# A gated short-convolution layer on one core: sums of a product with 128 equal columns, an eviction moved ahead of a cast, and the gate's loads moved behind the first stage

## The chip, the core and the metric

The kernel runs on one core of one Trainium2 chip. Five engines matter: TensorE (PE in the profile; PEld is its weight load), VectorE (DVE), ScalarE (ACT), GpSimd (POOL) and SyncE (SP), whose queue issues nearly all DMAs. Each engine works through its own instructions in order and waits for the others at semaphores. The metric is the device time of one execution in microseconds (us); less is better.

## What is computed

One layer on a sequence of 256 rows with 2048 features; everything is float32.

```python
def short_conv_mixer(h, w_in, conv_w, w_out):
    proj = jnp.einsum('bsd,de->bse', h, w_in)            # 2048 -> 4 x 4096
    b_gate, c_gate, v, g = jnp.split(proj, 4, axis=-1)
    u = causal_depthwise_conv(c_gate * v, conv_w)        # width 3
    y = b_gate * u * jax.nn.silu(g)
    return jnp.einsum('bse,ed->bsd', y, w_out)           # 4096 -> 2048

mod = jnp.einsum('bd,df->bf', jax.nn.silu(c), ada_w) + ada_b   # 2048 -> 3 x 2048
shift, scale, gate = jnp.split(mod, 3, axis=-1)
h = rmsnorm(x, norm_g) * (1.0 + scale) + shift
out = rmsnorm(x + gate * short_conv_mixer(h, ...), final_g)
```

Weights are read once: 128 MB of `w_in`, 32 MB of `w_out` and 48 MB of `ada_w`.

## The kernel before, in words

**Precision.** A float32 weight tile of 128 x 2048 (1 MB) is split in two: ScalarE casts it to a rounded part `hi`, VectorE subtracts to get the rest `lo`. The features are split in the same way into `hT` (high and low half). Each product of the layer is three matmuls: hi with high, hi with low, lo with high.

**Preamble (the first 26 us).** x is loaded and transposed on TensorE while `ada_w`'s columns for the first two feature tiles (k = 0 and 1) are loaded in 18 pieces. Their sums over 2048 rows, weighted with silu(c), make shift and scale of these two tiles. VectorE makes 13 of the 16 weighted additions (L391, into `gv0`); TensorE makes the other three (`ON_PE = (7, 11, 13)`, `sum0`, L377) as matmuls whose moving operand is one column, and at last adds `gv0` over the partitions with a column of ones. The results land in `sum0`, VectorE adds the bias (L424, `sh_sc`), ScalarE and VectorE make the features (`features`, L356 to L358), and the first product can start. Between these pieces stand matmuls that compute nothing (`idle`, L280, as many as the table `IDLE` says at eight places); they keep TensorE occupied. Three small loads on POOL's queue bring `norm_g`, all 48 rows of `ada_b` and 96 rows of `conv_w`; two transposes (`tp_v`, L266) turn them, one of them for `cw`, the convolution's taps.

**First stage (26 to 388 us).** It makes half of the projection, while shift and scale of the other 14 feature tiles are still being summed: `ada_w` comes in pieces `at` (512 KB each in two DMAs), VectorE adds them into `gv` (L475), TensorE turns a finished pair of tiles (`tp_g`, L482), ScalarE totals it (L489), VectorE makes scale and shift, and two more features appear in `hT`. The work is cut into 65 blocks (numbered 0 to 64): one weight tile `raw_s`, 48 matmuls (24 in blocks 0 and 1). Most blocks have two halves of 24 matmuls, each into its own PSUM tile (`mm_s`, called a bank in the code), and a pass of one to four blocks fills the same two. Three PSUM buffers rotate: a pass's half can start only when an earlier tile in its buffer has been evicted. Evictions are copies on ScalarE (L529, `acc<-mm_s`) or additions on VectorE (L531); a later pass of the same outputs may start from the evicted sums, which ScalarE copies back (L665, `mm_s<-acc`).

The order of the first stage is written out by the loop over `flat` (L715), with a small clock model that counts each engine's time. In the iteration of block b the loop emits, in this order: the cast `hi` of block b + 2 (L587, through `high`), the eviction of the second half of the pass that ended one block ago (`close_bank(ended_pass, ...)`, L529), some sums, `lo` of block b + 2 (L594), and then block b's matmuls; the first half's eviction is emitted between the two halves. Casts use three `hi` buffers and three `raw` buffers, so a cast waits for its load and for TensorE to leave a buffer. When all features are there, the pinned order ends and the scheduler orders what follows by itself.

**Second stage (388 to 737 us).** The other half of the projection, in 64 tiles of 1 MB with 48 matmuls each (`mm_b`). At every second tile the code issues one of 32 pieces of the gate's part of `ada_w` (`gate_piece`: load `at_g`, 512 KB, L792, and two additions into `gacc`, L799 and L801; after eight pieces TensorE adds over the partitions, `ps_gate`, L808). A lowered priority (`GIVE = 300`) lets the scheduler move them. Nothing they read ties them to the second stage, so it has placed all of them in the first stage's second half.

**Output stage (737 to 918 us).** y times `w_out` in four column groups, with gate, residual and final norm.

Of the kernel before, what the change touches and what calls it, by code (L numbers as in the profile page):

```python
# [49 lines left out]

RAW0 = 23.9
FIRST = 25.2
ISSUE_US = 2.0
TURN_US = 1.0
LOAD_US = 2.65
PIECE_US = 1.47
# [95 lines left out]
def short_conv_layer(ctx: ExitStack, tc: tile.TileContext, x, c, norm_g, ada_w, ada_b, w_in, conv_w, w_out, final_g, out):  # L152
    nc = tc.nc
# [69 lines left out]
    GIVE = 300  # L223
    IDLE = (2, 1, 3, 2, 2, 3, 7, 2)
    xt = [[slot([P, HX], f"x{t}{dh}") for dh in range(2)] for t in range(TT)]
# [8 lines left out]
    NK0 = ADA[0]  # L234
    first_ada = []
# [15 lines left out]
    nc.gpsimd.dma_start(rows1[0:16, :], norm_g.rearrange("o (k p) -> (o k) p", p=P))  # L251
    nc.gpsimd.dma_start(rows1[16:64, :], ada_b.rearrange("o (k p) -> (o k) p", p=P))
    nc.gpsimd.dma_start(rows2[:, :], conv_w.rearrange("w (k p) -> (w k) p", p=P))
    ones_e = const.tile([P, P], F32R, tag="ones", name="ones")
# [4 lines left out]

    vec = const.tile([P, 64], F32, tag="vec", name="vec")  # L260
    cw = const.tile([P, 96], F32, tag="cw", name="cw")
    silu_c = const.tile([P, KT], F32, tag="silu", name="silu_c")

    def turn(rows, lo, n, dst):
        tp = psum.tile([P, 512], F32, tag="sm", name="tp_v", bufs=2)[:, : n - lo]
        nc.tensor.transpose(tp, rows[lo:n, :], ident[lo:n, lo:n])  # L266
        if dst is not None:
            nc.vector.tensor_copy(dst, tp)
        return tp
# [16 lines left out]
    idle(0, turned[2])  # L286
    tp_v = turn(rows1, 0, 64, None)
    gT = vec[:, 0:16]
# [4 lines left out]
    idle(1, turned[2])  # L293
    tp_c = turn(rows2, 0, 96, None)
    idle(2, turned[2])
# [15 lines left out]
    nc.scalar.copy(vec, tp_v)  # L311
    nc.scalar.copy(cw, tp_c)
    nc.vector.tensor_tensor(out=rstd, in0=ssq[:, 0, :], in1=ssq[:, 1, :], op=ALU.add)
# [54 lines left out]

    ON_PE = (7, 11, 13)
    sums0 = [psum.tile([P, 512], F32, tag="sm", name="sum0", bufs=2) for _ in range(NK0)]  # L370
    gv0 = adap.tile([P, 2, 2 * P], F32, tag="gv", name="gv0")[:, :, 0 : NK0 * P]

    def sum0(k, rows, col):

        for f in range(NK0):
            for s in range(2):
                nc.tensor.matmul(  # L377
                    sums0[f][:, s : s + 1], rows[:, s, f * P : (f + 1) * P], col,
                    start=k == ON_PE[0] and s == 0, stop=k is None, skip_group_check=True,
                )  # L380

    def sum0_of(n):
        k = ON_PE[n]
        sum0(k, first_ada[k], silu_c[:, k : k + 1])

# [30 lines left out]
    idle(6, tp_idle)  # L416
    sum0(None, gv0, ones[:, 0:1])
    idle(7, tp_idle)
# [4 lines left out]
    for k in range(NK0):  # L423
        nc.vector.tensor_tensor(out=sh_sc[:, k], in0=sums0[k][:, 0:2], in1=b_both[:, :, k], op=ALU.add)  # L424
    for k in range(NK0):
# [124 lines left out]
    def spend(engine, us, since=0.0):  # L550

        clock[engine] = max(clock[engine], since) + us
        return clock[engine]

    def issue():

        while todo:
            free = [i for i, (kind, item) in enumerate(todo) if not held(kind, item)]
            if not free or free[0] and todo[free[0]][0] == "a":
                return  # L560
            kind, item = todo.pop(free[0])
            if kind == "w":
                _, chs, q, _, _, _, w, s0, sk, _ = flat[item]
                n = sk * w
                col = q * E + chs[0] * CT * P
                raws[item] = raw_tile("raw_s")
                nc.sync.dma_start(
                    raws[item][:, :n].rearrange("p (k f) -> p k f", k=sk),
                    w_in[0, s0 * P : (s0 + sk) * P, col : col + w].rearrange("(k p) f -> p k f", p=P),
                )  # L570
# [9 lines left out]
    def high(b):  # L580

        _, _, _, _, _, _, w, _, sk, _ = flat[b]
        n = sk * w
        while b not in raws:
            sum_one()
        hi = wpool.tile([P, SLOT], F32R, tag="hi", name="hi", bufs=3)
        nc.scalar.copy(hi[:, :n], raws[b][:, :n])  # L587
        spend("act", HI_US * n / SLOT, raws.pop((b, "at")))
        return hi, n, clock["act"]
# [125 lines left out]
    for b, (n, chs, q, k0, k1, seeds, w, s0, sk, _) in enumerate(flat):  # L715
# [257 lines left out]
```

## Time and profile before

| what | value |
|---|---|
| median of three runs | 920.33 us (917.95 to 921.09) |
| the profiled execution's own time | 920.34 us |
| its span on the core | 918.6 us |
| TensorE busy | 900.2 us (98 %) |
| VectorE busy | 632.3 us (69 %) |
| ScalarE busy | 454.1 us (49 %) |
| DMA, mean over the span | 248 GB/s |

In a row of the timeline the columns are start and duration in us, engine, line and operation, the tiles written and read, partitions x elements, the count of instructions merged, and in brackets how long the engine had been idle and what ended the wait. TensorE is busy nearly all the time, so what counts is the few places where it is not, and the 26 us before its first product of the layer.

### The profile page before, as it was taken

To read this page: it belongs to the slowest core of one execution; us is meant where nothing else is said; L and a number is where in the kernel's file an instruction comes from. 1 tells how busy PE (TensorE), PEld (TensorE's weight loads), DVE (VectorE), ACT (ScalarE), POOL (GpSimd) and SP (SyncE) were. 2 spreads that over 40 slices of the span, in tenths; PEclk is the share of its full clock that TensorE was granted. 3 is DMA by queue.
4 is the path that set the end of the run, shared out by engine and by line. 5 is a ranking of instruction groups with operands and counts; after the bars stand their busy time and mean duration, and the time that the engine had idled before them with its cause. 6 is when DMAs were issued, how large, how long until landed. Compare 5 with 4: busy or idle time off the path is not lost.

```text
span 918.6 us, 16218 instructions
## 1 busy us (share of the span) xinstructions
PE 900.2 (98%) x7043; PEld 861.0 (94%) x7043; DVE 632.3 (69%) x603; ACT 454.1 (49%) x431; POOL 2.3 (0%) x9
## 2 busy tenths in 40 slices
PE   7999999999999999999999999999999999999996
PEld 4899999999999999999999999999999988888885
DVE  5888899999988999985545554555454544545882
ACT  6677776545544766543444334433344333443333
POOL 1000000000000000000000000000000000000000
PEclk9999999999999999999999999999999999999999
DMA  9999899999998669876666656665666496555542
GB/s 304 372 382 351 295 355 354 317 351 325 349 337 313 210 216 359 250 247 187 188 197 201 195 183 194 198 204 186 186 192 198 143 343 222 191 203 202 183 138 91
DMA packets 146775, 227.64 MB, mean 248 GB/s; under 512 B 5456, under 2 KB 103808, under 8 KB 146320
## 3 DMA queue, kind: packets, MB, share of 16 engines
q1 hardware_dynamic: 146576, 226.51, 73.1%
q8 instruction: 55, 0.90, 0.4%
q14 instruction: 16, 0.13, 0.0%
q0 software_dynamic: 96, 0.08, 0.0%
q10 hardware_dynamic: 32, 0.01, 0.0%
HBM read 224.49 MB, written 2.10 MB: 247 GB/s over the span
## 4 chain that ended last, share of the span: by engine, by line
PE 92%; DMA 5%; ACT 1%; DVE 1%; issue 0%; ACTq 0%; SPq 0%; DVEq 0%
PE mm_b L497 38%; PE mm_s L497 35%; PE mm_o L869 6%; PE mm_o L871 6%; PE mm_o L870 6%; DMA at<-in_ada_w_dram 2%; DMA raw_s<-in_sc_w_in_dram 2%; DMA at_g<-in_ada_w_dram 1%; ACT hi L587 1%; DMA x<-in_x_dram 1%; DVE lo L594 0%; PE tp_g L482 0%; ACT acc L529 0%; DVE acc L434 0%; DVE gv L475 0%
## 5 line engine op out<-in xcount | busy, mean ns | idle before, releaser
L497 PE MATMUL mm_b<-hT,hi 128*128 128x256 f32 x2048 | 348.4, 276 | 0.0
L497 PE MATMUL mm_s<-hT,hi 128*128 128x256 f32 x2048 | 338.0, 277 | 3.8 <-ACT acc L529 3.8
L497 PEld LDWEIGHTS mm_b<-hT,hi 128*128 128x128 f32 x2048 | 308.2, 188 | 0.0
L497 PEld LDWEIGHTS mm_s<-hT,hi 128*128 128x128 f32 x2048 | 299.9, 188 | 5.0 <-ACT acc L529 4.3
L497 PE MATMUL mm_b<-hT,lo 128*128 128x256 f32 x1024 | 282.6, 276 | 0.0
L497 PE MATMUL mm_s<-hT,lo 128*128 128x256 f32 x1024 | 262.7, 277 | 1.3 <-DVE lo L594 1.3
L365 DVE TENSOR_TENSOR lo<-raw,hi 128x2048 fp32r<-128x2048 f32 x64 | 146.7, 2293 | 133.0 <-ACT hi L364 133.0
L364 ACT CAST hi<-raw 128x2048 fp32r<-128x2048 f32 x64 | 122.5, 1913 | 196.2 <-PE mm_b L497 149.9
L497 PEld LDWEIGHTS mm_b<-hT,lo 128*128 128x128 f32 x1024 | 192.2, 188 | 0.1
L497 PEld LDWEIGHTS mm_s<-hT,lo 128*128 128x128 f32 x1024 | 183.1, 188 | 1.8 <-DVE lo L594 1.7
L587 ACT CAST hi<-raw_s 128x2048 fp32r<-128x2048 f32 (+1 forms) x64 | 121.5, 1900 | 111.5 <-PE mm_s L497 90.7
L594 DVE TENSOR_TENSOR lo<-raw_s,hi 128x2048 fp32r<-128x2048 f32 (+1 forms) x64 | 145.4, 2272 | 19.1 <-ACT hi L587 18.5
L365 DVE TENSOR_TENSOR lo<-raw_o,hi 128x2048 fp32r<-128x2048 f32 x32 | 73.3, 2291 | 64.6 <-ACT hi L364 64.6
L364 ACT CAST hi<-raw_o 128x2048 fp32r<-128x2048 f32 x32 | 61.0, 1907 | 106.8 <-PE mm_o L871 84.8
L870 PE MATMUL mm_o<-lo,y 128*128 128x512 f32 x256 | 99.3, 389 | 0.0
L871 PE MATMUL mm_o<-hi,y 128*128 128x512 f32 x256 | 99.3, 389 | 0.0
L869 PE MATMUL mm_o<-hi,y 128*128 128x512 f32 x256 | 99.3, 389 | 0.0
L475 DVE SCALAR_TENSOR_TENSOR gv<-at,silu_c,gv 128x512 f32<-128x512 f32 x105 | 78.7, 750 | 2.5
L871 PEld LDWEIGHTS mm_o<-hi,y 128*128 128x128 f32 x256 | 48.0, 188 | 10.1
L870 PEld LDWEIGHTS mm_o<-lo,y 128*128 128x128 f32 x256 | 48.0, 188 | 10.0
L869 PEld LDWEIGHTS mm_o<-hi,y 128*128 128x128 f32 x256 | 48.1, 188 | 9.8
L801 DVE SCALAR_TENSOR_TENSOR gacc<-at_g,silu_c,gacc 128x512 f32<-128x512 f32 x60 | 44.9, 748 | 8.7 <-DMA at_g<-in_ada_w_dram 7.9
(107 smaller groups left out, 378.6 us busy)
## 6 DMA issues: line engine op xcount, KB each, us to landing
raw<-in_sc_w_in_dram SPq DMA_DIRECT2D x64, 1024.0 KB, 5.6
raw_s<-in_sc_w_in_dram SPq DMA_DIRECT2D x63, 1024.0 KB, 7.3
raw_o<-in_sc_w_out_dram SPq DMA_DIRECT2D x32, 1024.0 KB, 5.2
at<-in_ada_w_dram SPq DMA_DIRECT2D x126, 256.0 KB, 7.1
at_g<-in_ada_w_dram SPq DMA_DIRECT2D x32, 512.0 KB, 6.3
x<-in_x_dram SPq DMA_DIRECT2D x4, 512.0 KB, 6.5
big<-in_x_dram SPq DMA_DIRECT2D x2, 1024.0 KB, 7.8
out_dram<-big SPq DMA_DIRECT2D x4, 512.0 KB, 2.9
```

The lines of the kernel that those rows point to most:

```text
L364: nc.scalar.copy(hi[:, :n], raw[:, :n])
L365: nc.vector.tensor_tensor(out=lo[:, :n], in0=raw[:, :n], in1=hi[:, :n].bitcast(F32), op=ALU.subtract)
L475: nc.vector.scalar_tensor_tensor(out=gv, in0=at4[:, i], scalar=c_k, in1=gv, op0=ALU.mult, op1=ALU.add)
L497: mm = last_mm[0] = nc.tensor.matmul(dst, w, h[:, k], start=begins and left, stop=ends, skip_group_check=True)
L587: nc.scalar.copy(hi[:, :n], raws[b][:, :n])
L594: nc.vector.tensor_tensor(out=lo[:, :n], in0=raws.pop(b)[:, :n], in1=hi[:, :n].bitcast(F32), op=ALU.subtract)
L801: nc.vector.scalar_tensor_tensor(out=ga, in0=at3[:, i, :], scalar=s, in1=ga, op0=ALU.mult, op1=ALU.add)
L869: nc.tensor.matmul(po, yh, hi[:, o], start=opens, stop=False, skip_group_check=True)
L870: nc.tensor.matmul(po, yh, lo[:, o], start=False, stop=False, skip_group_check=True)
L871: nc.tensor.matmul(po, yl, hi[:, o], start=False, stop=ct == NCT - 1, skip_group_check=True)
```

## The change

Five edits:

1. The first sums on TensorE take 128 equal columns (silu(c)'s column broadcast, or `ones`) as moving operand instead of one; a fourth row tile (k = 15) is summed on TensorE, so VectorE makes 12 additions instead of 13. The two feature tiles' sums are ordered one after the other. The `IDLE` table changes from 22 to 15 matmuls in all.
2. `conv_w`'s rows are loaded and turned after block 44 (`CONV_AT`), on SP's queue; of `ada_b` 32 rows are loaded early instead of 48.
3. The second half's eviction of an ended pass is emitted before the cast of block b + 2 when the model expects that block's load late (`early`).
4. The gate's loads get an ordering dependency on the last `raw_s` load of the first stage.
5. The model's two start times `RAW0` and `FIRST` are 1.0 and 1.2 us less, which moves four of the seven `tp_g` by one block.

```diff
-RAW0 = 23.9
-FIRST = 25.2
+RAW0 = 22.9
+FIRST = 24.0
+EARLY_US = 2.0
+CONV_AT = 44
...
-    IDLE = (2, 1, 3, 2, 2, 3, 7, 2)
+    IDLE = (2, 2, 3, 2, 2, 2, 1, 1)
...
-    nc.gpsimd.dma_start(rows1[16:64, :], ada_b.rearrange("o (k p) -> (o k) p", p=P))
-    nc.gpsimd.dma_start(rows2[:, :], conv_w.rearrange("w (k p) -> (w k) p", p=P))
+    nc.gpsimd.dma_start(rows1[16:48, :], ada_b[0:1, 0 : 2 * D].rearrange("o (k p) -> (o k) p", p=P))
...
-    tp_c = turn(rows2, 0, 96, None)
...
-    nc.scalar.copy(cw, tp_c)
...
-    ON_PE = (7, 11, 13)
-    sums0 = [psum.tile([P, 512], F32, tag="sm", name="sum0", bufs=2) for _ in range(NK0)]
+    ON_PE = (7, 11, 13, 15)
+    sums0 = [psum.tile([P, 2, 2 * P], F32, tag="sm", name="sum0", bufs=2)[:, :, 0:P] for _ in range(NK0)]
...
+        for s in range(2):
+            nc.tensor.matmul(
+                sums0[f][:, s, :], rows[:, s, f * P : (f + 1) * P], cols,
+                start=k == ON_PE[0] and s == 0, stop=k is None, skip_group_check=True,
+            )
+
+    def sum_of(n, f):
+        k = ON_PE[n]
+        sum0(k, f, first_ada[k], silu_c[:, k : k + 1].to_broadcast([P, P]))
...
-    sum0(None, gv0, ones[:, 0:1])
+    for f in range(NK0):
+        sum_of(3, f)
+        sum0(None, f, gv0, ones)
...
-        nxt = b + 2 < N and high(b + 2)
-        if ended_pass is not None:
-            close_bank(ended_pass, len(passes[ended_pass][1]) - 1)
-            ended_pass = None
+        early = b + 2 < N and raws.get((b + 2, "at"), begin) > begin - EARLY_US
+        for closing in (early, not early):
+            if closing:
+                if ended_pass is not None:
+                    close_bank(ended_pass, len(passes[ended_pass][1]) - 1)
+                    ended_pass = None
+            else:
+                nxt = b + 2 < N and high(b + 2)
...
+        if b == CONV_AT:
+            nc.sync.dma_start(rows2[:, :], conv_w.rearrange("w (k p) -> (w k) p", p=P))
+            turn(rows2, 0, 96, cw)
...
-        nc.sync.dma_start(at3, adas[:, j : j + 2, 2, dc * 512 : (dc + 1) * 512])
+        at = nc.sync.dma_start(at3, adas[:, j : j + 2, 2, dc * 512 : (dc + 1) * 512])
+        tc.add_manual_dep(at.ins, last_load[0].ins.name, after, reason="behind the first stage's loads")
```

How the instructions move, at three places. On TensorE, the end of the preamble, before (`tp_idle` are the matmuls that compute nothing, `gv0` VectorE's sum, `at0_109` the last loaded rows):

```order
L377 MATMUL sum0_174<-silu_c_133,at0_109 128x1 x2
L377 MATMUL sum0_175<-silu_c_133,at0_109 128x1 x2
L280 MATMUL tp_idle_246<-ones_r_137 128x512 x7
L377 MATMUL sum0_174<-ones_127,gv0_176 128x1 x2
L377 MATMUL sum0_175<-ones_127,gv0_176 128x1 x2
L280 MATMUL tp_idle_246<-ones_r_137 128x512 x2
```

and with the change:

```order
L375 MATMUL sum0_172<-silu_c_132,at0_109 128x128 x2
L281 MATMUL tp_idle_242<-ones_r_136 128x512
L375 MATMUL sum0_171<-silu_c_132,at0_109 128x128 x2
L375 MATMUL sum0_171<-ones_126,gv0_173 128x128 x2
L375 MATMUL sum0_172<-silu_c_132,at0_109 128x128 x2
L375 MATMUL sum0_172<-ones_126,gv0_173 128x128 x2
L281 MATMUL tp_idle_242<-ones_r_136 128x512
```

Seven of the nine matmuls without a result are gone there (7 became 1, 2 became 1), four products of the fourth row tile are new, and the first feature tile's sum is complete before the second one's begins.

On ScalarE, blocks 2 to 6, before (`hi_310` is block 2's cast, `hi_341` block 3's, `hi_381` block 4's, `hi_446` block 5's; `mm_s_309` and `mm_s_316` are the PSUM tiles of blocks 0 and 1, `mm_s_355` and `mm_s_356` block 2's two halves):

```order
L587 CAST hi_310<-raw_s_287 128x2048
L587 CAST hi_341<-raw_s_292 128x2048
L529 COPY acc01_343<-mm_s_309 128x1024
L587 CAST hi_381<-raw_s_301 128x2048
L529 COPY acc11_383<-mm_s_316 128x1024
L529 COPY acc02_419<-mm_s_355 128x1024
L587 CAST hi_446<-raw_s_314 128x2048
```

and with the change (`hi_302`, `hi_335`, `hi_375` and `hi_440` are the same four casts, `mm_s_301`, `mm_s_308`, `mm_s_347` and `mm_s_348` the same PSUM tiles):

```order
L593 CAST hi_302<-raw_s_279 128x2048
L533 COPY acc01_333<-mm_s_301 128x1024
L593 CAST hi_335<-raw_s_284 128x2048
L533 COPY acc11_373<-mm_s_308 128x1024
L593 CAST hi_375<-raw_s_293 128x2048
L533 COPY acc02_411<-mm_s_347 128x1024
L533 COPY acc12_438<-mm_s_348 128x1024
L593 CAST hi_440<-raw_s_306 128x2048
```

The evictions of blocks 0 and 1 and of each second half stand one cast earlier; the first half's (`mm_s_347`) still follows block 4's cast.

On VectorE, around block 37, where the last pair of feature tiles is summed, before (`gv_2389` is that sum, `gacc_4549` the gate's, `at_g` the gate's loads):

```order
L594 TENSOR_TENSOR lo_2648<-raw_s_2447,hi_2646 128x2048
L475 SCALAR_TENSOR_TENSOR gv_2389<-at_2451,silu_c_133,gv_2389 128x512 x2
L475 SCALAR_TENSOR_TENSOR gv_2389<-at_2456,silu_c_133,gv_2389 128x512
L799 TENSOR_SCALAR gacc_4549<-at_g_4547,silu_c_133 128x512
L475 SCALAR_TENSOR_TENSOR gv_2389<-at_2456,silu_c_133,gv_2389 128x512
L801 SCALAR_TENSOR_TENSOR gacc_4549<-at_g_4547,silu_c_133,gacc_4549 128x512
L594 TENSOR_TENSOR lo_2706<-raw_s_2524,hi_2704 128x2048
L475 SCALAR_TENSOR_TENSOR gv_2389<-at_2536,silu_c_133,gv_2389 128x512
L801 SCALAR_TENSOR_TENSOR gacc_4549<-at_g_4662,silu_c_133,gacc_4549 128x512
L475 SCALAR_TENSOR_TENSOR gv_2389<-at_2536,silu_c_133,gv_2389 128x512
```

and with the change:

```order
L600 TENSOR_TENSOR lo_2638<-raw_s_2433,hi_2636 128x2048
L479 SCALAR_TENSOR_TENSOR gv_2435<-at_2438,silu_c_132,gv_2435 128x512 x2
L479 SCALAR_TENSOR_TENSOR gv_2435<-at_2443,silu_c_132,gv_2435 128x512 x2
L600 TENSOR_TENSOR lo_2696<-raw_s_2498,hi_2694 128x2048
L479 SCALAR_TENSOR_TENSOR gv_2435<-at_2504,silu_c_132,gv_2435 128x512 x2
L479 SCALAR_TENSOR_TENSOR gv_2435<-at_2509,silu_c_132,gv_2435 128x512 x2
L600 TENSOR_TENSOR lo_2754<-raw_s_2580,hi_2752 128x2048
```

The gate's additions no longer stand between those of the last pair. All 64 of them now follow the load of block 64's weights on SP's queue, and on VectorE they lie between `lo` of block 62 and about the 27th tile of the second stage.

More of the change, by code (lines that the diff above doesn't have):

```diff
@@ L258, in short_conv_layer @@
     nc.vector.memset(eps_t, EPS)
-    vec = const.tile([P, 64], F32, tag="vec", name="vec")
+    vec = const.tile([P, 48], F32, tag="vec", name="vec")
     cw = const.tile([P, 96], F32, tag="cw", name="cw")
@@ L286, in short_conv_layer @@
     idle(0, turned[2])
-    tp_v = turn(rows1, 0, 64, None)
+    tp_v = turn(rows1, 0, 48, None)
     gT = vec[:, 0:16]
@@ L366, in split, with sum0, sum0_of @@
         return hi, lo
-    ON_PE = (7, 11, 13)
-    sums0 = [psum.tile([P, 512], F32, tag="sm", name="sum0", bufs=2) for _ in range(NK0)]
+    ON_PE = (7, 11, 13, 15)
+    sums0 = [psum.tile([P, 2, 2 * P], F32, tag="sm", name="sum0", bufs=2)[:, :, 0:P] for _ in range(NK0)]
     gv0 = adap.tile([P, 2, 2 * P], F32, tag="gv", name="gv0")[:, :, 0 : NK0 * P]
-    def sum0(k, rows, col):
-        for f in range(NK0):
[L376 to L384, printed above, removed]
+    def sum0(k, f, rows, cols):
+        for s in range(2):
[6 more added lines that the diff above has]
+        sum0(k, f, first_ada[k], silu_c[:, k : k + 1].to_broadcast([P, P]))
+    def sum0_of(n):
+        for f in range(NK0):
+            sum_of(n, f)
     for k in range(KT):
@@ L423, in short_conv_layer @@
     for k in range(NK0):
-        nc.vector.tensor_tensor(out=sh_sc[:, k], in0=sums0[k][:, 0:2], in1=b_both[:, :, k], op=ALU.add)
+        nc.vector.tensor_tensor(out=sh_sc[:, k], in0=sums0[k][:, :, 0], in1=b_both[:, :, k], op=ALU.add)
     for k in range(NK0):
@@ L553, in spend @@
         return clock[engine]
+    last_load = [None]
     def issue():
@@ L566, in issue @@
                 raws[item] = raw_tile("raw_s")
-                nc.sync.dma_start(
+                last_load[0] = nc.sync.dma_start(
                     raws[item][:, :n].rearrange("p (k f) -> p k f", k=sk),
```

## The prediction

> **What bounds the kernel now.** I began with the page's chain of work that ended last, then asked what TensorE waits for, and then went through its timeline stage by stage.
>
> ```profile
> PE 92%; DMA 5%; ACT 1%; DVE 1%; issue 0%; ACTq 0%; SPq 0%; DVEq 0%
> ```
>
> TensorE itself is 92 % of the chain. A change that adds no product and removes none can therefore only shift TensorE's first product or close one of its gaps. The waits of TensorE after its start are few:
>
> ```profile
> PE mm_s L497 <- ACT acc L529: 3.8, 3, 1.9
> ```
>
> Three waits for evictions on ScalarE, 3.8 us in all, are the largest row; one for `lo` (1.3 us) and one for the sums of a pair (0.8 us) are met below in the timeline. All five lie in the first stage. Everything else is product after product. Times below are of the one profiled execution (920.34 us, 0.01 from the median of the three runs); about 0.3 %, 2.8 us, is what a measurement of this kernel can tell from no change.
>
> **The start.** The last sums on TensorE and the two results of VectorE that follow:
>
> ```profile
> 19.75 1.03 PE L334 MATMUL tp_x<-ident,x 128*128 128x128 f32 x8
> ```
> ```profile
> 21.66 2.33 DVE L391 SCALAR_TENSOR_TENSOR gv<-at,silu_c,gv 128x512 f32<-128x512 f32 x3 [0.59 <-DMA at<-in_ada_w_dram]
> ```
> ```profile
> 23.03 1.86 PE L280 MATMUL tp_idle<-ones_r 128*128 128x512 f32 x7
> 24.72 0.95 PE L377 MATMUL sum<-ones,gv 128*128 128x1 f32 x8
> ```
> ```profile
> 25.71 0.16 DVE L424 TENSOR_TENSOR sh_sc<-sum,vec 128x2 f32<-128x2 f32 x1 [0.29 <-PE sum L377]
> ```
>
> `gv0` is done at 21.66 + 2.33 = 23.99, but TensorE is in its seven matmuls without result until 24.7. A sum with one column takes 0.95 / 8 = 0.119 us, a transpose with 128 columns 1.03 / 8 = 0.129 us: the wider operand costs next to nothing (bounds 0 and 8 x 0.01). After the change VectorE ends one addition earlier (2.33 / 3 = 0.78), at 23.21. The last rows must have landed when their addition began in the row above, 23.2, at the latest; TensorE then has sixteen passes of 0.119 us, four for each tile's last rows and four for each tile's `gv0`. From 23.2 the second tile's sum ends at 23.2 + 1.9 = 25.1 instead of 25.67 (-0.55); if the rows land 0.3 earlier, which the order of the loads lets me expect, at 24.8 (-0.86). The first tile's sum gains more, about 1.1 us, but the second tile's features are what the third group of products needs, so I take **-0.86** with -0.55 as the other end. The removed matmuls and `tp_c` otherwise stood in waits for loads. This gain doesn't simply arrive, as the next part shows.
>
> **Blocks 2 and 3: the moved evictions.**
>
> ```profile
> 32.83 1.92 ACT L587 CAST hi<-raw_s 128x2048 fp32r<-128x2048 f32 x1 [2.35 <-DVE lo L594]
> 34.65 1.00 ACT L529 COPY acc<-mm_s 128x1024 f32<-128x1024 f32 x1
> 36.88 1.91 ACT L587 CAST hi<-raw_s 128x2048 fp32r<-128x2048 f32 x1 [1.23 <-DMA raw_s<-in_sc_w_in_dram]
> 38.70 1.92 ACT L529 COPY acc<-mm_s 128x1024 f32<-128x1024 f32 x2
> ```
> ```profile
> 35.70 2.10 PE L497 MATMUL mm_s<-hT,hi 128*128 128x256 f32 x16 [0.78 <-ACT acc L529]
> 37.64 1.07 PE L497 MATMUL mm_s<-hT,lo 128*128 128x256 f32 x8
> 39.75 2.10 PE L497 MATMUL mm_s<-hT,hi 128*128 128x256 f32 x16 [1.04 <-ACT acc L529]
> 41.68 1.07 PE L497 MATMUL mm_s<-hT,lo 128*128 128x256 f32 x8
> 42.59 1.98 PE L497 MATMUL mm_s<-hT,hi 128*128 128x256 f32 x16
> ```
>
> A half of 24 products takes 42.59 - 39.75 = 2.84 us here; a row's end stands some 0.15 past the next unhindered start (41.68 + 1.07 = 42.75 against 42.59). So the second wait costs 39.75 - (35.70 + 2.84) = 1.21 us and the first about 0.78 + 0.1 = 0.88. In both the cast stood ahead of the eviction on ScalarE, and the second of these casts waited for its load. With the evictions ahead, both waits go: -0.88 - 1.21, with the start -2.95, and block 3's second half would begin at 42.59 - 2.95 = 39.64.
>
> But that half needs another eviction, that of block 2's first half, which the order of ScalarE still shows behind block 4's cast (`hi_375`, then `mm_s_347`). That cast began at 36.88, 0.1 after its load; cast and copy end at 38.70 + 0.96 = 39.66, and TensorE can go on at 39.75. Nothing in the change makes that load earlier: the small loads that leave the preamble are given back by `conv_w`'s rows (48 KB, 0.14 us at the 346 GB/s of this stretch), which the scheduler puts just ahead of it on SP. So the half begins at 39.75: **-2.84** for start and evictions together, whichever way the start comes out between -0.75 and -1.2 (at -0.55 it would be -2.64); the load itself may move by 0.3 either way.
>
> ```profile
> 26.00:226.00 200.00, 196.24 (x1707) 195.24 (x1706) 178.19 (x198) 133.32 (x151) 0.00 (x0) 1.00 0.99 346
> ```
>
> The windows' last columns here are clock, DMA share (0.99) and GB/s.
>
> **Block 9: a wait that takes their place.** Its second product needs the low half of the features of k = 2, which VectorE makes behind `lo` of block 10, itself behind the cast on ScalarE:
>
> ```profile
> 67.73 1.91 ACT L587 CAST hi<-raw_s 128x2048 fp32r<-128x2048 f32 x1
> ```
> ```profile
> 69.67 2.29 DVE L594 TENSOR_TENSOR lo<-raw_s,hi 128x2048 fp32r<-128x2048 f32 x1 [0.30 <-ACT hi L587]
> ```
> ```profile
> 72.32 0.43 DVE L358 TENSOR_TENSOR hT<-xs,hT 128x256 fp32r<-128x256 f32 x1
> ```
> ```profile
> 68.41 2.04 PE L497 MATMUL mm_s<-hT,hi 128*128 128x256 f32 x16
> ```
> ```profile
> 74.06 2.04 PE L497 MATMUL mm_s<-hT,hi 128*128 128x256 f32 x16
> ```
>
> Today the feature is there at 72.75, 1.4 us before its use at 74.17. After the change block 8 begins at 68.41 - 2.84 = 65.57; only then can block 7's second half be evicted, and the cast now stands behind that eviction: 66.0 (its last product and the release, an estimate) + 1.0, cast to 68.8, `lo` to 71.1, feature at 71.1 + 0.8 = 71.9, wanted at 74.17 - 2.84 = 71.33. That is **+0.55** (bounds 0, if the casts catch up, and 0.8).
>
> **Block 11: a wait that stays.**
>
> ```profile
> 85.26 1.91 ACT L587 CAST hi<-raw_s 128x2048 fp32r<-128x2048 f32 x1 [1.36 <-PE mm_s L497]
> ```
> ```profile
> 88.92 1.01 ACT L529 COPY acc<-mm_s 128x1024 f32<-128x1024 f32 x1
> ```
> ```profile
> 89.99 0.51 PE L497 MATMUL mm_s<-hT,hi 128*128 128x256 f32 x2 [1.94 <-ACT acc L529]
> ```
>
> Between these two rows ScalarE makes two more copies, 1.0 us each: cast and three copies, 4.8 us from the moment TensorE hands the bank over. The change only puts the cast behind the first copy. The last copy, which block 11's second half waits for, keeps all four ahead of or in itself: **0** (bounds -2.05, its whole price, and 0).
>
> **The gate's loads.**
>
> ```profile
> 233.66 0.75 DVE L801 SCALAR_TENSOR_TENSOR gacc<-at_g,silu_c,gacc 128x512 f32<-128x512 f32 x1 [1.97 <-DMA at_g<-in_ada_w_dram]
> ```
> ```profile
> 235.12 0.66 PE L482 MATMUL tp_g<-ident,gv 128*128 128x128 f32 x4 [0.82 <-DVE gv L475]
> ```
> ```profile
> 315.41 0.74 DVE L801 SCALAR_TENSOR_TENSOR gacc<-at_g,silu_c,gacc 128x512 f32<-128x512 f32 x1
> 316.07 1.66 DVE L434 SCALAR_TENSOR_TENSOR acc<-acc,cw,acc 128x254 f32<-128x254 f32 x4
> ```
> ```profile
> 319.99 0.39 PE L497 MATMUL mm_s<-hT,lo 128*128 128x256 f32 x1 [1.30 <-DVE lo L594]
> ```
>
> At 233.66 a gate addition waited 1.97 us for its load, with the last pair's sum queued behind it, and TensorE's `tp_g` behind that. With no gate addition there (the third excerpt of the order), and `tp_g` a block later, the wait goes: -0.82 - 0.1 = **-0.92**. At 320 `lo` was late on a VectorE full of taps (0.41 us each) and gate additions, each 0.66 from its start to the next one's; the one at 315.41 and the one some 5 us before it are as much as the wait. Gone: -1.30 - 0.1 = **-1.40**. What is late next in both places is only the next product.
>
> ```profile
> 226.00:388.00 162.00, 159.88 (x1403) 159.12 (x1402) 149.82 (x170) 92.83 (x91) 0.00 (x0) 1.00 0.83 290
> 388.00:560.00 172.00, 172.00 (x1520) 172.00 (x1519) 97.39 (x78) 72.44 (x56) 0.00 (x0) 1.00 0.65 202
> ```
> ```profile
> L801 DVE SCALAR_TENSOR_TENSOR gacc<-at_g,silu_c,gacc x60: 740/748/754, 228.1 to 386.8; 128x512 f32<-128x512 f32 x60
> ```
>
> The third number of a window's busy times is VectorE: 149.82 of 162 us (92 %) from 226 to 388, 97.39 of 172 (57 %) after. The 64 additions, 48 us at 0.748, now fall into about 27 tiles of the second stage, 27 x 48 x 0.1133 = 147 us: 0.57 x 147 + 48 = 131 us, 89 %. That is nearer to the full stretch than to the easy one, and the full one cost two waits, 2.3 us. But `lo` is far ahead of its use here:
>
> ```profile
> 222.57 2.29 DVE L594 TENSOR_TENSOR lo<-raw_s,hi 128x2048 fp32r<-128x2048 f32 x1 [0.77 <-ACT hi L587]
> ```
> ```profile
> 231.65 0.28 PE L497 MATMUL mm_s<-hT,lo 128*128 128x256 f32 x1
> ```
>
> It was ready at 224.86 for a product at 231.65, 6.8 us ahead, near the end of the first stage; three additions or a late load don't use that up. I take **+0.3** (bounds 0 and 2.3).
>
> **`conv_w`'s transpose** leaves the preamble, where TensorE waited for loads anyway, for the start of block 45, where each moment counts.
>
> ```profile
> 11.42 0.37 PE L266 MATMUL tp_v<-ident,rows 96*128 96x96 f32 x1
> ```
>
> It took 0.37 us there; a turn of a pair of sums, four of them, takes 0.66 (above). I take **+0.2** (bounds 0.1 and 0.4). Its copy on VectorE hides under that engine's lead.
>
> **Sum:** -2.84 + 0.55 + 0 - 0.92 - 1.40 + 0.3 + 0.2 = -4.11, so 920.34 - 4.11 = **916.2 us**.
>
> **Rivals.**
> *Block 11's wait goes too.* If the shifted casts let ScalarE reach the last copy 2 us sooner: -2.1, 914.1 us. For it: TensorE comes earlier, so do loads. Against it: the chain starts when TensorE releases the bank. 12 %.
> *Loads set the early pace.* DMA share is 0.99 up to 226 us; if block 4's load and those behind it come late, half of the 2.84 is given back: 917.6 us. 13 %.
> *The change doesn't do what it says at 320:* the taps that stand around the gate's additions (four of them 1.66 us, above) make `lo` late by themselves. +1.4, 917.6 us. 10 %.
> *The clock drops.*
>
> ```profile
> 12.49 0.34 PEld L280 LDWEIGHTS tp_x<-ones_r 128*128 128x128 f32 x1 [0.52 <-issue]
> 13.34 0.23 PEld L280 LDWEIGHTS tp_x<-ones_r 128*128 128x128 f32 x1 [0.52 <-issue]
> 13.81 0.19 PEld L280 LDWEIGHTS tp_x<-ones_r 128*128 128x128 f32 x1 [0.24 <-issue]
> ```
>
> The same matmul steps by 0.85 us up to 13.34 and by 0.47 after it: TensorE starts slow (from 26 us on the windows' clock column above reads 1.00). With seven matmuls fewer around the last sums it could fall back for a stretch such as its first, 9.55 to 13.34 or 3.8 us, at half the products: 1.9 us late. Since block 3 has 0.1 us of slack and block 9's wait would vanish, that gives about +1, 917.2 us. Against it, TensorE's new pauses are shorter than 1.3 us each. 8 %.
> [...]
> *VectorE becomes the bound of the second stage* (slower). Its spare time in the 147 us is 16 us, the lead 6.8: from 22.6 us of waiting at the gate's loads on, TensorE loses. Today they are few:
>
> ```profile
> DVE gacc L801 <- DMA at_g<-in_ada_w_dram: 7.9, 5, 2.2
> ```
>
> If each second of the 32 loads made it wait the longest, 2.2, that is 35 us; TensorE loses 12 and the time is about 928 us. 4 %.
>
> **How the numbers follow.** The forecast, 916.2 within 1.2, has 47 %; the rivals 12, 13, 10, 8 and 4; 6 % is none of these. From 913.6 to 918.6 lie nearly all of the first five: 8 in 10. Faster by 0.3 % means under 917.57: the forecast, block 11's case, half of the three near 917.5 and some of the rest, 78 %. Within 0.3 %: 18 %; slower: 4 %.
>
> **What would show it.** First product near 25.1; no idle ahead of block 2's second half and block 3's first; block 3's second half near 39.75 right behind a copy on ScalarE; a wait of about half a us in block 9 and one near 2 in block 11; no `gacc` before the last `raw_s` load, no idle at 232 and 317; VectorE near 90 % from 385 to 530 and TensorE without a gap there. The prediction is wrong if block 4's load lands elsewhere than at 36.8, if TensorE's products after the start step by more than 0.12 us, or if the second stage shows gaps.

## The result: slower by 4.2 %

| | before | after |
|---|---|---|
| median of six runs | 918.38 us (917.32 to 921.09) | 956.96 us (955.94 to 962.07) |
| ratio, 95 % interval | | 1.0422 (1.0395 to 1.045) |
| profiled execution, its span | 918.6 us | 954.3 us |
| first product of the layer | 26.17 us | 23.91 us |
| first stage, from there | 361.8 us | 372.6 us |
| second stage | 348.7 us | 370.9 us |
| output stage, to the last product | 174.8 us | 179.8 us |

The stages run from the first product (`mm_s`, `mm_b`, `mm_o`) of each to the first of the next in the timeline. The start came out early and every stage after it longer, the output stage too, in which the change moves nothing. So the first place to look is what all stages share. From the page of the changed kernel, the chain and the groups of the second stage's products (count, then busy time and mean ns of one):

```profile
PE 82%; DMA 11%; DVE 4%; issue 1%; ACT 1%; SPq 0%; ACTq 0%; DVEq 0%
...
L501 PE MATMUL mm_b<-hT,hi 128*128 128x256 f32 x2048 | 366.8, 282 | 0.0
```

and the same group on the page of before:

```profile
L497 PE MATMUL mm_b<-hT,hi 128*128 128x256 f32 x2048 | 348.4, 276 | 0.0
```

The same 2048 products take 18 us longer. (TensorE's share of the chain fell from 92 to 82 % because the chain now runs through the gate's loads and VectorE for a while; that turns out to be the smaller part.) Three stretches without any wait, one in each stage, first of before and then of after (stretch, us, TensorE's busy time and the count of its matmuls in it; clock, DMA share and GB/s at the end):

```profile
250.00:310.00 60.00, 60.00 (x532) 60.00 (x531) 51.52 (x54) 31.25 (x28) 0.00 (x0) 1.00 0.85 299
580.00:680.00 100.00, 100.00 (x885) 100.00 (x884) 53.50 (x40) 40.20 (x31) 0.00 (x0) 1.00 0.63 197
800.00:900.00 100.00, 100.00 (x443) 82.81 (x442) 67.59 (x43) 37.91 (x28) 0.00 (x0) 1.00 0.51 171
```

```profile
250.00:310.00 60.00, 60.00 (x506) 60.00 (x505) 32.87 (x27) 28.48 (x26) 0.00 (x0) 1.00 0.53 177
580.00:680.00 100.00, 100.00 (x840) 99.91 (x839) 51.02 (x37) 37.54 (x28) 0.00 (x0) 1.00 0.59 184
800.00:900.00 100.00, 100.00 (x431) 80.12 (x430) 54.23 (x34) 37.83 (x28) 0.00 (x0) 1.00 0.56 189
```

TensorE is busy from end to end in all six, at a granted clock of 1.00, and yet gets through 506 instead of 532, 840 instead of 885, 431 instead of 443. From start to start of neighbours, a product of the projection takes 119.1 ns after and 113.3 before (second stage), one of the output stage, twice as wide, 233.3 and 226.7. That is 6 to 7 ns for each, not a fixed share of its time. 6144 x 5.8 ns + 768 x 6.6 ns = 40.7 us; before had already spent 1.7 us of that in its own slow spells (below), so 39 us are new. This is more than the whole loss.

What is left of the 35.9 us between the last products: the start gives back 2.3 us, waits of the first stage that are gone give 5.4, and the second stage takes 4.5 us beyond its slower products. The waits of TensorE in the changed kernel show part of that (the first row):

```profile
PE mm_b L501 <- DVE lo L364: 2.2, 4, 1.3
PE mm_s L501 <- ACT acc L533: 1.9, 1, 1.9
```

In before no product of the second stage waited for `lo`.

**A suspect.** No line of the change touches a product of the layer. But `vec`, a small tile of constants, became 48 columns wide instead of 64, which the list of five edits and the diff above leave out. The program's allocation of the on-chip memory (SBUF) puts everything behind it 64 bytes lower: the pieces of `ada_w`, and the buffers `lo`, `hi` and `raw`, in which the layer's weights lie. `hT` and `y` come from the other end and stay. A product reads two operands there and stands in the trace as two rows: LDWEIGHTS on PEld for the operand of 128 columns, called loaded here (188 ns in the mean for `mm_b` with `hi`, page of before), and MATMUL on PE, as wide as the other, called moving, with 256 or 512 columns (276 ns for the same `mm_b`). In both projection stages `hi` or `lo` is loaded and `hT` moves; in the output stage `y` is loaded and `hi` or `lo` moves (`matmul(po, yh, hi[:, o])`). "The weights" below are `hi` and `lo` in either part. The kernel has unused tiles (`line`, `line0`, `line2`, `line3`) at just these borders, which the prediction passed over. And the trace of before shows that products don't always go at one pace:

```profile
52.00:64.00 12.00, 12.00 (x104) 12.00 (x104) 10.61 (x12) 9.69 (x8) 0.00 (x0) 1.00 1.05 386
106.00:122.00 16.00, 16.00 (x143) 16.00 (x142) 15.11 (x15) 12.11 (x11) 0.00 (x0) 1.00 0.91 318
```

A stretch also counts a matmul at each of its ends that lies only partly in it; without those it is 118 ns a product from 52 to 64 us and 113 from 106 to 122, both without a wait.

### The profile page after: what moved, and what is told of

It reads as the page before. It is cut to its first block, busy times and chain, and to the rows that moved or that the text cites. A ratio compares the mean times of both kernels' runs of the same rounds, so it can differ in the third digit from the quotient of the medians.

```text
span 954.3 us, 16213 instructions
## 1 busy us (share of the span) xinstructions
PE 938.0 (98%) x7045; PEld 893.4 (94%) x7045; DVE 633.5 (66%) x603; ACT 452.8 (47%) x430; POOL 1.8 (0%) x8
## 4 chain that ended last, share of the span: by engine, by line
PE 82%; DMA 11%; DVE 4%; issue 1%; ACT 1%; SPq 0%; ACTq 0%; DVEq 0%
PE mm_s L501 37%; PE mm_b L501 25%; DMA at_g<-in_ada_w_dram 9%; PE mm_o L884 6%; PE mm_o L883 6%; PE mm_o L885 6%; DVE gacc L815 2%; DVE lo L364 2%; DMA x<-in_x_dram 1%; DVE gv L479 0%; DMA at<-in_ada_w_dram 0%; PE sum L375 0%; ACT hi L593 0%; PE tp_g L486 0%; PE tp_x L333 0%
## 5 line engine op out<-in xcount | busy, mean ns | idle before, releaser
L501 PE MATMUL mm_b<-hT,hi 128*128 128x256 f32 x2048 | 366.8, 282 | 0.0
L501 PE MATMUL mm_s<-hT,hi 128*128 128x256 f32 x2048 | 353.7, 283 | 2.1 <-ACT acc L533 1.9
L501 PEld LDWEIGHTS mm_b<-hT,hi 128*128 128x128 f32 x2048 | 315.3, 189 | 0.0
L501 PEld LDWEIGHTS mm_s<-hT,hi 128*128 128x128 f32 x2048 | 306.5, 189 | 2.9 <-ACT acc L533 2.1
L501 PE MATMUL mm_b<-hT,lo 128*128 128x256 f32 x1024 | 289.0, 282 | 2.3 <-DVE lo L364 2.2
L501 PE MATMUL mm_s<-hT,lo 128*128 128x256 f32 x1024 | 268.0, 282 | 0.1
L883 PE MATMUL mm_o<-hi,y 128*128 128x512 f32 x256 | 100.5, 394 | 0.0
L885 PE MATMUL mm_o<-hi,y 128*128 128x512 f32 x256 | 100.5, 394 | 0.0
```

The lines of the kernel that those rows point to most:

```text
L501: mm = last_mm[0] = nc.tensor.matmul(dst, w, h[:, k], start=begins and left, stop=ends, skip_group_check=True)
L883: nc.tensor.matmul(po, yh, hi[:, o], start=opens, stop=False, skip_group_check=True)
L885: nc.tensor.matmul(po, yl, hi[:, o], start=False, stop=ct == NCT - 1, skip_group_check=True)
```

## Experiments: the place of the weights

Two theories: the place of the buffers decides the pace (P), or the slow pace is a state that TensorE enters in its first passes and that the pauses of before happened to end (S). `line0` can move all weights and nothing else; each engine's instructions stay as they are.

**e1**: the changed kernel, weights 64 bytes up, where before has them.

```diff
-    const.tile([P, 32], F32, tag="line0", name="line0")
+    const.tile([P, 48], F32, tag="line0", name="line0")
```

> The changed kernel; an unused tile in front of the buffers is 48 instead of 32 columns wide, so the pieces of ada_w and the weight buffers hi, lo and raw lie 64 bytes higher, where the kernel before had them; every engine's instructions are the same. Theory P (place): the narrower vec moved the weights by 64 bytes and each product pays for that (0.119 us against 0.1133). Then products go at 0.113 again, 6144 x 5.8 ns + 768 x 6.6 ns = 41 us come back, and the time is 914 to 918 us. Rival S (state): the slow pace is a state that TensorE enters at its first products and left, in the kernel before, only because of the pauses at 35, 39 and 88 us that the change removes or shifts; then this kernel stays at 0.119 and 955 to 958 us.

Measured: 927.65 us, 1.008 (1.0057 to 1.0102) of before. 29 us are back; products go at 113.5 ns in the second stage and 226.7 in the output stage. But it is still slower than before, by a part that P doesn't explain; it lies in the second stage alone and has its own section.

**e2**: the kernel before, weights 64 bytes down (`line0` 16 columns wide).

> The kernel before, the unused tile 16 instead of 32 columns wide: the same buffers 64 bytes lower, as the change has them; instructions the same. P: products at 0.119 us through all stages, and 918 + 39 = 955 to 960 us. S: it stays at 0.113 and 917 to 921 us, since its pauses are all there.

Measured: 955.15 us, 1.0377 (1.0353 to 1.0401). One unused tile, made 64 bytes smaller, costs the tuned kernel 35 us. Its windows have the counts of the changed kernel:

```profile
250.00:310.00 60.00, 60.00 (x506) 60.00 (x505) 51.29 (x52) 27.02 (x20) 0.00 (x0) 1.00 0.86 301
580.00:680.00 100.00, 100.00 (x842) 100.00 (x842) 50.24 (x36) 37.56 (x28) 0.00 (x0) 1.00 0.59 182
800.00:900.00 100.00, 100.00 (x430) 80.55 (x430) 54.88 (x33) 37.89 (x28) 0.00 (x0) 1.00 0.57 190
```

S by itself is out: e2 has before's instructions and is slow in all three windows; e1 has the change's and gets through 531, 883 and 443 in the same three. (A state does play a part, as e4 shows below.) The clock is out as well, it reads 1.00 in every window shown here.

What of the place counts? **e3** moves the changed kernel's weights up by 32 bytes, **e4** down by 64 (`line0` 40 and 16 columns); **e7** leaves them and moves `hT` up by 64 (`line` 40, `line2` 64 columns, so that `y` stays); **e8** moves `hi` and `raw` up by 64 but not `lo` (`line3` 48 columns).

> The changed kernel with the buffers 32 bytes higher. P says nothing exact: if only one multiple of 128 bytes is bad, products go at 0.113 and it takes 914 to 918 us; if 64 past a multiple of 128 is the good place, they stay at 0.119 (955 to 958) or lie between. S: 955 to 958.

> The changed kernel with the buffers 64 bytes lower than it has them: 64 past a multiple of 128 again, as in the kernel before, but 128 bytes off its place (448 and 320 past a multiple of 512 instead of 64 and 448). P, if the place counts by 128: 914 to 918 us. P, if it counts by 512 or by the distance to hT and y: 955 or between. S: 955 to 958.

> The changed kernel with its weights where the change put them, and the features hT 64 bytes higher instead (y, the output stage's moving operand, not moved); instructions the same. If the distance between weights and moving operand counts: the first two stages at 0.113 us a product, the output stage still at 0.233 (in place of 0.227), about 957 - 36 + 7 (VectorE's waits grow to e1's) = 926 to 932 us. If only the weights' own place counts: 0.119 everywhere, 954 to 958.

> The changed kernel with hi and raw 64 bytes higher and lo (as used in the two projection stages) where the change put it; the output stage takes both its weight parts from the buffers that moved. If each weight tile's own place counts, the products with hi (two in three) go at 0.113, those with lo at 0.119, the output at 0.227: about 935 to 942 us. If hi and lo must both lie right, 0.119 in the two stages and 0.227 in the output: 948 to 953. If lo doesn't count: 927 to 932.

Measured: 957.33, 944.7, 944.82 and 947.87 us (one run each). e4 lies between the two paces' times, as its text allows for a count by 512 or by the distance. e7 and e8 miss: e7 lies between the ranges of both theories, e8 just below its 948. e4 and e7 have their tiles in different places, yet the same time; what they share is how far the weights lie past `hT`, counted by 512 bytes (a row of 128 weights). (Where the expectation of e7 calls `y` the moving operand of the output stage, it is the loaded one; this changes nothing of what was moved.)

The windows of e4 show that its time is no pace of its own, but two paces in one run:

```profile
300.00:400.00 100.00, 100.00 (x885) 100.00 (x884) 86.56 (x98) 62.17 (x62) 0.00 (x0) 1.00 0.69 232
620.00:720.00 100.00, 100.00 (x842) 99.92 (x841) 49.95 (x37) 38.83 (x29) 0.00 (x0) 1.00 0.60 187
```

The first count is that of before, the second that of e2. From 300 to 480 us products go at 113.3 ns, from 620 to 740 at 118.9, and e7 does the same at nearly the same times. In the second stage about half of the products go at either pace, so 116.1 ns is only their mean. Two of the changes stand within a few products of an interruption: a wait for `lo` at 486, the gate's matmuls `ps_gate` at 606. So at this distance TensorE held either pace in one run, for 180 us the one and for 120 us the other.

The shared distance made a last test possible, **e11**: the kernel before with no weight moved, only `hT` 64 bytes up, so that these distances become those of the change.

> The kernel before with weights and y where they are and hT 64 bytes higher, so that hi and lo lie 256 and 128 bytes past hT, counted by 512, as the change made them, though no weight has moved. If this distance decides (as e4 and e7 suggest: other places, the same distances 192 and 64, and 944.7 and 944.8 us): products at 0.119 in both projection stages, at 0.227 in the output stage, 918.4 + 34 = 950 to 956 us. If the weights' own place decides: 917 to 921.

Measured: 950.76 us, slow in the projection and not in the output stage, as the distance has it:

```profile
250.00:310.00 60.00, 60.00 (x506) 60.00 (x506) 52.71 (x54) 27.59 (x20) 0.00 (x0) 1.00 0.91 322
580.00:680.00 100.00, 100.00 (x842) 100.00 (x841) 50.73 (x36) 37.57 (x28) 0.00 (x0) 1.00 0.59 184
800.00:900.00 100.00, 100.00 (x443) 82.84 (x442) 58.00 (x36) 39.61 (x29) 0.00 (x0) 1.00 0.59 194
```

All of them together, with the mean step of a product where nothing waits (distances counted by 512 bytes; the output stage takes both its `hi` and its `lo` from places with the same remainder):

| kernels | `hi` and `lo` past `hT`, bytes | second stage, ns | `hi` and `lo` past `y`, bytes | output stage, ns |
|---|---|---|---|---|
| before, e1 | 320, 192 | 113.3, 113.5 | 0 | 226.7 |
| after, e2 | 256, 128 | 119.1 | 448 | 233.3 |
| e11 | 256, 128 | 119.1 | 0 | 226.7 |
| e3 | 288, 160 | 118.3 | 480 | 233.3 |
| e4 | 192, 64 | 113.3 and 118.9 | 384 | 232.5 |
| e7 | 192, 64 | 113.3 and 118.9 | 448 | 233.3 |
| e8 | 320, 128 | 118.2 | 0 | 226.7 |

Rows with the same distances agree, whatever else differs: the weights moved and `hT` stayed (e2), or `hT` moved and the weights stayed (e11), and both step by 119.1 ns. So in these runs the distance between the two operands decides which paces occur, and the place of either one alone has nothing left to explain. In e8, with `hi` where it is good and only `lo` moved, the step from one `hi` product to the next is slow too (119.0 ns); so a product's pace isn't set by its own weights alone. Which distances are good, and why, stays open: 0 and 64 past a multiple of 128 are good in one stage and bad in the other. That the count goes by 512 isn't shown either; 256 would fit these runs as well, 128 would not (before and e4 are alike by 128).

Moving one of the two operands against the other by 64 bytes changed each product by 5.8 ns (113.3 in before, 119.1 in e2 and e11).

## Experiments: the gate's additions

e1 has products at full pace and takes 360.0 us for the second stage instead of 348.7. Its windows of the stage, with VectorE's busy time as the third number, and VectorE's waits for the gate's loads and TensorE's for `lo`:

```profile
384.00:455.00 71.00, 71.00 (x629) 71.00 (x628) 56.00 (x60) 30.90 (x25) 0.00 (x0) 1.00 0.86 278
455.00:532.00 77.00, 69.99 (x588) 67.73 (x587) 56.08 (x58) 25.05 (x21) 0.00 (x0) 1.00 0.81 257
532.00:744.00 212.00, 212.00 (x1868) 211.81 (x1868) 114.30 (x83) 88.39 (x66) 0.00 (x0) 1.00 0.63 194
```

```profile
DVE gacc L815 <- DMA at_g<-in_ada_w_dram: 21.7, 13, 3.2
...
DVE gacc L813 <- DMA at_g<-in_ada_w_dram: 8.1, 3, 3.4
```

```profile
PE mm_b L501 <- DVE lo L364: 7.0, 10, 1.4
```

For 71 us all is well; then the lead of `lo` is used up and TensorE loses time until the last addition at 532. VectorE is busy for only 73 % of that stretch (56.08 of 77): it isn't too much work, it is waiting, 29.8 us in all since 365. Its timeline (e1) shows how:

```profile
467.91 0.75 DVE L815 SCALAR_TENSOR_TENSOR gacc<-at_g,silu_c,gacc 128x512 f32<-128x512 f32 x1
470.87 1.54 DVE L815 SCALAR_TENSOR_TENSOR gacc<-at_g,silu_c,gacc 128x512 f32<-128x512 f32 x2 [2.21 <-DMA at_g<-in_ada_w_dram]
472.33 2.29 DVE L364 TENSOR_TENSOR lo<-raw,hi 128x2048 fp32r<-128x2048 f32 x1
```

TensorE waits for that `lo` until 474.67. An addition whose load isn't there holds back the next tile's `lo`. That `lo` also frees the `raw` buffer for the next load on SP's queue, so the loads behind it probably come later as well; no run tests this link by itself.

**e5**: e1 with the fourth edit undone.

```diff
-        at = nc.sync.dma_start(at3, adas[:, j : j + 2, 2, dc * 512 : (dc + 1) * 512])
-        tc.add_manual_dep(at.ins, last_load[0].ins.name, after, reason="behind the first stage's loads")
+        nc.sync.dma_start(at3, adas[:, j : j + 2, 2, dc * 512 : (dc + 1) * 512])
```

> The changed kernel with the buffers 64 bytes up (as in e1) and the gate's loads without their new ordering dependency, so that the gate's 64 additions stand in the first stage again. In e1 the second stage took 360.0 us against 348.7 before, with 10 waits of TensorE for lo. Theory G (the moved additions, which wait 29.8 us in all for their loads with lo queued behind them, cost those 11.4 us): the second stage takes 349 us again, up to 2.3 us of waits return in the first stage, and the time is 916 to 919 us. Rival (something else of the change lengthens the second stage): it stays at 360 and the time at 926 to 930.

Measured: 918.98 us, 0.9995 (0.9978 to 1.0012): the second stage takes 348.6 us again, and the first ends at 386.09 instead of e1's 384.37. The total can't be told from that of before: what start and evictions gain shows in the trace alone.

Not all of e1's 11.4 us is waiting. With the additions, two pairs of the gate's matmuls (`ps_gate`) moved from the first stage into the second, where each pair lengthens a tile by 0.49 us, 1.0 us in all; e9 below has this 1.0 us as well.

**e6**: e1 with each gate load ordered behind the load of its own tile (the raw load's handle kept in `last_load[0]` at every tile), spread over all 64 tiles.

> e1 with each of the 32 gate loads ordered behind the raw load of its own tile in the second stage (one load for two tiles, over all 64) instead of behind the first stage's last load (all 32 within the first 27 tiles). G: VectorE gets 48 us of additions spread over 349 us instead of 147, and the second stage takes 349 to 351 us; nothing returns to the first stage: 915 to 918 us. If already a few waits behind a late load cost TensorE (and not their density), it stays above 920.

Measured: 958.27 us, 1.0425 (1.0378 to 1.0472). My expectation was wrong by 42 us, and this tells most about the mechanism: less than half as many additions per microsecond, and five times the waiting.

```profile
DVE gacc L815 <- DMA at_g<-in_ada_w_dram: 150.2, 28, 7.3
```
```profile
499.14 2.29 DVE L364 TENSOR_TENSOR lo<-raw,hi 128x2048 fp32r<-128x2048 f32 x1
508.16 0.75 DVE L815 SCALAR_TENSOR_TENSOR gacc<-at_g,silu_c,gacc 128x512 f32<-128x512 f32 x1 [6.73 <-DMA at_g<-in_ada_w_dram]
508.82 0.68 DVE L852 TENSOR_TENSOR z<-mm_b,z 128x512 f32<-128x512 f32 x1
509.43 0.74 DVE L815 SCALAR_TENSOR_TENSOR gacc<-at_g,silu_c,gacc 128x512 f32<-128x512 f32 x1
510.08 2.28 DVE L364 TENSOR_TENSOR lo<-raw,hi 128x2048 fp32r<-128x2048 f32 x1
```

The wait for the load comes ahead of a `lo` whose cast had ended at 500.46. VectorE waits so for 31 of the 32 pieces; why the scheduler put the additions there isn't shown.

**e9**: e6 with each addition ordered behind `lo` of the tile whose load its own load follows.

```diff
+            tc.add_manual_dep(add.ins, last_lo[0].ins.name, after, reason="behind this tile's lo")
```

> e6 (buffers 64 bytes up, one gate load for two tiles of the second stage) with one more ordering: the gate's two additions of a piece stand behind lo of the tile whose raw load the piece's load follows, so some 16 us behind that load's issue, instead of ahead of it. In e6 VectorE waited 160 us in 31 waits for gate loads, with lo queued behind. Theory W (the price is the wait of an addition that stands ahead of lo, whatever the density): the waits go, the second stage takes 349 to 351 us, 914.5 to 917.5 us in all, faster than the kernel before by about 0.3 %. If the additions' number in the second stage costs by itself: 920 or more.

Measured: 916.64 us, 0.9964 (0.995 to 0.9978). No addition waits for its load any more, the second stage takes 349.6 us, and this version is faster than both kernels, than before by 0.4 %. Its row for the same place in the stage:

```profile
477.18 2.29 DVE L366 TENSOR_TENSOR lo<-raw,hi 128x2048 fp32r<-128x2048 f32 x1 [2.54 <-ACT hi L365]
479.39 1.53 DVE L817 SCALAR_TENSOR_TENSOR gacc<-at_g,silu_c,gacc 128x512 f32<-128x512 f32 x2
482.62 2.29 DVE L366 TENSOR_TENSOR lo<-raw,hi 128x2048 fp32r<-128x2048 f32 x1 [1.70 <-ACT hi L365]
```

## Experiment: the evictions

**e10**: e5 without the third edit.

```diff
-        early = b + 2 < N and raws.get((b + 2, "at"), begin) > begin - EARLY_US
+        early = False
```

> e5 without the third edit: each second half's eviction stands behind the cast of block b + 2 again. By the prediction's second term the waits ahead of block 2's second half and block 3's first half return (0.8 and 1.0 us idle), the one in block 9 goes: the first stage ends about 1.5 us later than in e5 (386.1), at 387 to 388.5, and the time is 919.5 to 921.5 us. If the moved evictions are worth nothing, it ends at 386 and the time is 919.

Measured: 926.49 us (one run), 5 us above the expected range, first stage to 394.26. The two waits are back where the prediction has them:

```profile
35.52 2.12 PE L501 MATMUL mm_s<-hT,hi 128*128 128x256 f32 x16 [0.49 <-ACT acc L533]
37.48 1.07 PE L501 MATMUL mm_s<-hT,lo 128*128 128x256 f32 x8
39.87 2.10 PE L501 MATMUL mm_s<-hT,hi 128*128 128x256 f32 x16 [1.32 <-ACT acc L533]
```

Block 4 starts at 45.46 instead of e5's 42.85, and block 10, with block 9's wait gone in turn, at 78.68 instead of 76.81: 1.9 us, near the 1.5 expected. The rest of the 8.2 us by which the first stage ends later is no price of the waits for evictions: the kernel's clock model, fed with other eviction times, placed the sums of a pair of feature tiles later (TensorE turns them at 99.96 instead of 92.74), and TensorE waits twice for `hT` (idle 2.4 and 2.0 us, at 103 to 108). So the evictions' own price is shown in the first 80 us only.

## Why the prediction was wrong

**The pace of a product: the step that failed.** The prediction held that a change that adds and removes no product "can therefore only shift TensorE's first product or close one of its gaps". It took 0.1133 us a product as given ("Everything else is product after product") and costed the narrower `vec` at nothing, without a word. That moved the weights against `hT` and `y` and cost 39 us (e1, e2, e11). Its closing test ("step by more than 0.12 us") was even set just beyond what came, 0.119. Two things in the material could have warned: before's stretch from 52 to 64 us at 118 ns, which the prediction passed over, and unused tiles in the code that only set places. That the distance is the cause is shown; why a distance is slow is not.

**The gate's additions in the second stage: a mis-sized term.** +0.3 us (bounds 0 and 2.3) measured 11.4 at full pace (e1) and 4.5 in the changed kernel, of which 1.0 each is the moved `ps_gate` matmuls. The waiting is much the same in both (29.8 and 28.4 us); that slower products ask for `lo` less often would explain the smaller loss, but isn't tested. The rival "VectorE becomes the bound" had it at 4 %: 22.6 us of waiting as the point from which it decides, 12 us lost at 35 us of waiting. By that sum e1's 29.8 us would have cost 7.2, and they cost about 10: the direction was right and the price still too low. What failed was the choice: I judged the waits rare by five of them in the first stage (7.9 us), where the additions lay among other work, and trusted 6.8 us of lead. The lead is spent once; the waits recur, 16 times in e1.

**What held.** With both causes repaired, e9's 916.64 us stands 0.4 beside the predicted 916.2. That it is so close is partly luck: e9 is another kernel than the predicted one, the runs of before beside it have a median of 919.98 us, so that e9 gains 3.3 us and not 4.1, and a wait for features in block 14 that costs 0.6 us stands in no term of the sum. The terms, one by one:

- Start and evictions, -2.84, by block 3's second half near 39.75: in e9 it begins, without a wait, at 39.88 and block 4 at 42.71, against 42.59 and 45.34 before (-2.7). The copy that the prediction has it wait for ended there near 39.7, just in time; in e5 TensorE does wait 0.37 us for it. In the changed kernel itself block 4's cast began at 35.47, not near 36.9, so that load isn't fixed as the prediction took it to be:

```profile
39.88 2.04 PE L503 MATMUL mm_s<-hT,hi 128*128 128x256 f32 x16
41.77 1.10 PE L503 MATMUL mm_s<-hT,lo 128*128 128x256 f32 x8
42.71 1.46 PE L503 MATMUL mm_s<-hT,hi 128*128 128x256 f32 x11
```

- First product: predicted near 25.1. The ten profiled executions with the new start have it at 23.91 to 25.75, 25.05 in the mean; the three with the old one (before, e2, e11) at 24.92 to 26.17, 25.67 in the mean. Two executions differ by more than the edit brings.
- Block 9's new wait: predicted 0.55; idle 0.48 in e9, ahead of the second product:

```profile
71.10 0.28 PE L503 MATMUL mm_s<-hT,hi 128*128 128x256 f32 x1
71.86 1.31 PE L503 MATMUL mm_s<-hT,hi 128*128 128x256 f32 x9 [0.48 <-DVE hT L357]
```

- Block 11's wait, predicted to stay near 2: in the changed kernel still

```profile
87.65 0.51 PE L501 MATMUL mm_s<-hT,hi 128*128 128x256 f32 x2 [1.91 <-ACT acc L533]
```

- The waits at 234 and 318 us: gone in after, e1 and e9 (-2.32 predicted). From before to e9 they give 1.0 us and, net of the 1.0 us of `ps_gate` matmuls that stood beside the second one, about 1.7. In e5, with the gate's additions back in the first stage, one of 1.5 us for `lo` and one of 1.0 for an eviction on VectorE are there again; e1's first stage ends 1.7 us earlier than e5's.
- `conv_w`'s transpose: +0.2 predicted; block 45 lasts 5.53 us in e9 against 5.44 of a full block without it: +0.1.

The clock rival is out: the clock column reads 1.00 in all windows shown, and the changed kernel's first four products take 0.72 us against 0.74 in before. That the slow start it builds on is the clock's isn't shown: the column reads 1.00 from 0 to 13 us of before too, where the matmul steps by 0.85 us. Nor did before fall back behind its longest wait in a stage, 1.94 us ahead of 89.99: the first steps there are 0.22 and 0.12 us.

## What to carry to other kernels

When an edit changes the size of any tile, compare the places of TensorE's two operands before and after, or hold them with padding: a 64-byte shift cost 4 % of the whole here, with a price in every stage and no instruction changed (e2). An addition that depends on a load belongs behind the work that TensorE waits for next, not ahead of it (916.64 us in e9, 958.27 in e6); spreading such additions out didn't help here while each still stood in front (e6). And where all stages lengthen by the same few per cent, count products per stretch before looking for waits.

## What the runs showed of the hardware

- In these runs a product's pace goes with the distance, in SBUF, between the loaded and the moving operand. In the mean, for 256 columns: 113.3 ns (before), 113.5 (e1), 118.2 (e8), 118.3 (e3), 119.1 (after, e2, e11); for 512: 226.7 (before, e1, e8, e11), 232.5 (e4), 233.3 (after, e2, e3, e7). The granted clock was 1.00 in every window shown, and 0.996 to 0.999 in the mean of each of these profiled executions.
- Two paces can occur at one distance. In before (113.3), products step by 114 to 123 ns for two to ten products behind a pause and then return (120, 117, 115, 115, then 113, behind the wait that ends at 39.75); from 51 to 80 us they stayed at 118. In e4 and e7 stretches at 113.3 and at 118.9 take turns; in e4 it is 113.3 from 300 to 480 us and 118.9 from 620 to 740. In after the products of both projection stages never return to 113: from 27 us to the end of the second stage any nine steps in a row have a median of 115 ns or more. What decides between return and no return isn't settled.
